# A two-layer decoder step on one core: a planner that tells a tile's first user from its writer, one more attention unit turned through DRAM, and output tiles entered between projections

## The chip, the core and the metric

The kernel runs on one core of a Trainium2 chip. The metric is the time on the device in microseconds (us), as the median of several executions. TensorE (PE) multiplies matrices out of SBUF into PSUM; VectorE (DVE), ScalarE (ACT) and GpSimd (POOL) work elementwise; SyncE (SP) issues nearly all transfers (DMAs), one behind the other in the order in which the program gives them.

## The reference

One inference step of a decoder for a prompt of 512 tokens and, with the same weights, for 8 sequences of one new token each, so 520 columns in all; the model width is 1024. The first layer is a gated linear recurrence (HGRN2, 16 heads of 128), the second is sliding-window attention (window 128, 32 query heads of 64, 4 key/value heads, partial rotary, a sink per head). Cut to what matters here:

```
# layer 0
u = rmsnorm(h, pre0) @ w_in_a;  q, f, i, z = split(u, 4)
o = hgrn2(silu(q), log f, 1 - f, i, S0)        # per head, chunked scan, final states are outputs
mix = (rmsnorm(o) * silu(z)) @ w_out_a
h = h + rmsnorm(mix, post0);  h = h + (p0 @ w_pe0) * sigmoid(h @ w_pg0)
# layer 1
k, v = split(rmsnorm(h, kvg) @ w_kv);  q, z = split(rmsnorm(h, pre1) @ w_in_b)
s = q k^T / 8, only keys of the last 128 positions;  pr = softmax([s, sink])[..., :-1]
mix = (pr v * silu(z)) @ w_out_b
h = h + rmsnorm(mix, post1);  h = h + (p1 @ w_pe1) * sigmoid(h @ w_pg1)
```

The outputs are h for both groups, the recurrent states, and the new key and value rows. All is float32; a product with a weight is made of three passes in the rounded format fp32r (high part of the weight by the high part of x, low part by high, high by low).

## The kernel before, in words

**Tiles.** A weight matrix is cut into tiles of 128 output rows. A tile is `kc` steps (8 for a projection) of six matmuls, for the two halves of 260 columns and the three passes. Weights arrive as `wr` (512 KB, 3 buffers); ACT rounds half of one to `wh`, and DVE or POOL makes the rest `wl`. Projection results stand in `pj` (2 pairs of PSUM banks), all else in `ph` (4 banks).

**Stages.** Embedding products; layer 0's 16 heads with four projections each (`proj_a`), each followed by that head's recurrence (`hgrn`), which runs beside the next heads' projections; after some heads a group's eight output tiles (`out_tiles`, groups in `GROUPS_A`: heads 0 to 3 after head 6, heads 4 to 7 after head 10, and so on). The last group goes by halves of the columns, and each half ends in a sum of squares `acc`, which `rstd` (L714) turns into the factors `R`: PE sums `acc` over the rows (`ones,acc`), DVE and POOL make `rsm` and `rsr`, PE spreads it by three or two transposes (`ident,rsr`), ACT copies it to `R`. `residual` (L777) then makes h and its parts `xs`, on which the `gates` tiles wait (weights `w_pg`). Layer 1 has eight units of four query heads: two query tiles and two gate tiles each (`unit_proj`), then the attention (`unit_attn`) beside the next units' projections, and groups of output tiles (`GROUPS_B`: units 0 and 1 after unit 4, units 2 and 3 after unit 5, units 4 and 5 after unit 7, then 6, then 7). It ends like layer 0.

**Attention of one unit** (`block`, L1327), in four blocks of 128 queries. W holds the scores, then the normalised weights (a buffer `b`, of the tags `b2` and `b3` with 3 buffers each). W has to be turned, queries to keys. For most units PE does that with four transposes into a bank, ACT rounds the bank to `hi`, DVE subtracts to get `lo`. For the units in `TURN_W` (4 and 5) `turn_weights` (L1414) does it: two DVE transposes of 32 by 32 blocks, one DMA to DRAM (`tw`), four DMAs back into W. In blocks 1 to 3 `hi` and `lo` are multiplied by a mask into two more tiles `ys`; in all units but the last two DMAs then move halves of the second into the first.

**Order.** Nothing is issued as it is written. `Plan.enter` (L187) records each operation with what it must follow; `Plan.issue` (L233) then builds the program by a list schedule with modelled costs: at each step the engine that can begin first takes, among the operations that are ready by the model, one by level (MAIN, SIDE, FIRST) and by its number in the written order. Operations further than `WINDOW`, for DMAs `LOADS`, from the lowest one that is not yet issued have to wait. The order in which each engine works is thus fixed before the run; on the chip an engine waits at each instruction for what it really needs. All instructions carry one line, that of the helper that calls them (L192).

`enter` makes an operation follow every earlier one that wrote a part of a tile which it reads or overwrites. It also makes each user of a tile follow the tile's first user, `self.maker[t]` (L211), whose output may be another part of the tile; `issue` counts that as a wait until the first user has ended, for a DMA until it has landed.

Of the kernel before, what the change touches and what calls it, by code (L numbers as in the profile page):

```python
# [9 lines left out]
F32 = mybir.dt.float32  # L10
F32R = mybir.dt.float32r
# [10 lines left out]
SEQ = 512  # L22
# [17 lines left out]
PIECE = 4 * P  # L40
SPLITS = 4
TURN_K, TURN_O = range(0, 15), range(1, 15)
TURN_W = (4, 5)
WARM = 17
BEHIND = 4

# [3 lines left out]
MAIN, SIDE, FIRST = 0, 1, 2  # L50
# [44 lines left out]
class Plan:  # L95
# [91 lines left out]
    def enter(self, on, name, a, k):  # L187
        outs = [k["accum_out"]] if "accum_out" in k else []
        outs.append(a[0])
        ins = [x for x in (*a, *k.values()) if isinstance(x, bass.AP)]  # L190
        calls = [getattr(getattr(self.nc, e), name) for e in on]
        op = Op(len(self.ops), self.level, on, [lambda c=c: c(*a, **k) for c in calls],  # L192
                [self.price(e, name, ins, a, k) for e in on], on[0] == "sync")
        if any(x.tensor.name.startswith("tw") for x in ins[1:]):
            op.late = LATE
        self.ops.append(op)
        for x in ins:
            t = x.tensor.name
            r = self.region(x)
            op.deps.update(o for q, o in self.writes.get(t, ()) if self.meet(q, r))  # L200
            self.reads.setdefault(t, []).append((r, op))
            kept = t in self.homes or x.space != bass.MemoryType.DRAM
            if kept and t not in self.left:
                tag, bufs = self.homes.get(t, (t, 1))
                if tag not in self.slots:
                    self.slots[tag] = Slots(tag, bufs)
                self.slots[tag].order.append(t)
                op.news.append((tag, t))
                self.maker[t] = op
            elif kept:  # L210
                op.deps.add(self.maker[t])  # L211
            if t not in op.tiles and kept:
                op.tiles.add(t)
                self.left[t] = self.left.get(t, 0) + 1
        for x in outs:
            t = x.tensor.name
            r = self.region(x)
            if on[0] == "tensor":
                r = 0, P, r[2] // 512 * 512, -(-r[3] // 512) * 512
            for book in (self.writes, self.reads):  # L220
                old = book.get(t, [])
                op.deps.update(o for q, o in old if o is not op and self.meet(q, r))
                book[t] = [(q, o) for q, o in old if o is op or not self.within(q, r)]
            self.writes.setdefault(t, []).append((r, op))
        op.deps.discard(op)
        op.load = op.dma and not op.deps
        for d in op.deps:
            d.users.append(op)
        op.open = len(op.deps)
        return op  # L230


    def issue(self):  # L233
# [3 lines left out]
        given, pipe, lanes, low, port, slow = set(), 0.0, [0.0] * 8, 0, 0.0, 0.0  # L237
        best = dict.fromkeys(clock)
        stale = set(clock)

        def after(d, e):

            if d.dma:
                return d.end + 0.1
            return d.end + (SAME if d.engine == e else LAT)[d.engine]

        def ready(op, e):
            return max((after(d, e) for d in op.deps), default=0.0)

        def place(op):  # L250
            at = 0.0
# [9 lines left out]
        def choose(e):  # L261
            able = []
            for op, r in wait[e]:
                p = place(op) if op.n < low + (LOADS if op.dma else WINDOW) else None
                if p is not None:
                    held = port if op.cost[op.on.index(e)][1] else 0.0
                    if op.dma and op.load and clock[e] > CALM and pipe > BACKLOG + op.cost[0][0]:
                        held = pipe - BACKLOG - op.cost[0][0]
                    able.append((max(r, p, clock[e], held), op, max(r, p)))
            if not able:  # L270
                return None
            t = min(x[0] for x in able)
            rank = RANK.get(e, OTHER)
            able = [x for x in able if x[0] <= t]
            safe = SAFE if t > CALM and low < self.second else 0.0
            fresh = lambda op: any(d.dma and d.end + safe > t for d in op.deps)
            able.sort(
                key=lambda x: (
                    e == "tensor" and x[2] + HAND > t or e in SHY and fresh(x[1]), rank[x[1].level], x[1].n
                )  # L280
            )
            if e == "gpsimd":
                for x in able:
                    op = x[1]
                    if len(op.on) > 1:

                        free = [
                            o.cost[0][0]
                            for o, r in wait["vector"]
                            if r <= t and not o.cost[0][1] and place(o) is not None  # L290
                        ]
                        if max(clock["vector"] - t, 0.0) * (port <= t) + sum(free) < op.cost[1][0]:
                            continue
                    return x
                return None
            return able[0]
# [6 lines left out]
        while todo:  # L303
# [11 lines left out]
            if op.n == low:  # L315
                while low < len(self.ops) and self.ops[low].engine:
                    low += 1
                stale.update(clock)
            cost, held = op.cost[n]
            if op.dma:  # L320
                t = max(t, lanes[0])
# [69 lines left out]
def in_turn(tiles):  # L391

    for t in tiles[1::2]:
        t.apart = True
    return tiles


def bank_of(ps, h):
# [56 lines left out]
class Step:  # L455
# [871 lines left out]
    def block(self, u, st, n, osb):  # L1327
# [52 lines left out]
                nc.tensor.matmul(po, base[0][:, kvh % 2], w, start=x == 0, stop=x == 1)  # L1380
        else:

            ys = [self.g_(F32R, SEQ) for x in range(2)]
            by = lambda x: x.rearrange("p (i h t) -> p i h t", h=4, t=run)
            mask = spot(self.tmask, 0, (run, P // run), (0, 4), (1, run))
            for x, y in zip((hi, lo), ys):
                nc.either.tensor_tensor(by(y), by(x.bitcast(F32)), mask, op=ALU.mult)
            y, z = (x.bitcast(F32) for x in ys)
            if u < 7:
                nc.sync.dma_start(y[HD:, : 4 * HD], z[:HD, : 4 * HD])  # L1390
                nc.sync.dma_start(y[:HD, 4 * HD :], z[HD:, 4 * HD :])
# [158 lines left out]
    def run(self):  # L1550
# [66 lines left out]
        def done_a(h):  # L1617
# [6 lines left out]

            return f

        for h in range(HEADS):
            tiles += self.proj_a(h, xg if h == 0 else xn, sts[h], done_a(h), R0 if h == 0 else None)
            if h + 1 in groups:
                tiles += out_a(h + 1)  # L1630
        tiles += out_a(17)
        end = out_a(18) + self.embed(0, pe[0], range(E0, KC), kept[0]) + self.embed(1, pe[1], range(E1))

# [47 lines left out]
        for u in range(8):  # L1681
            def done(u=u):
                self.beside(lambda: self.unit_attn(u, us[u]))
                if u % 4 == 3:
                    self.beside(lambda: self.sample_out(u // 4, us[u - 3 : u + 1]), FIRST)

            mine = self.unit_proj(u, qx, us[u], done)
            if u == 7:

                tiles[-2:-2] = mine[:2]  # L1690
                mine = mine[2:]
            tiles += mine
            if u + 1 in ogroups:
                tiles += out_b(u + 1)
        tiles += out_b(9)
        end1 = out_b(10) + self.embed(1, pe[1], range(E1, KC), kept[1])

# [143 lines left out]
```

## Time and profile before

| what | us |
|---|---|
| median of 3 runs | 1068.3 |
| lowest and highest of them | 1067.65, 1070.68 |
| the profiled execution's own time | 1068.61 |
| its span, first to last instruction | 1066.8 |
| PE busy, as the profile models it | 1057.2 |
| DVE busy | 904.7 |
| ACT busy | 681.8 |
| POOL busy | 114.0 |

Matmuls overlap in their pipeline, so that a row's mean duration (285 ns for most) is no cost; the distance from one start to the next is. Idle time of an engine counts only where the end of the program waits for it. Rows are grouped by what is written and read (`pj<-xs,wh`), with buffer numbers left out.

### The profile page before, as it was taken

To read this page: it belongs to the slowest core of one execution; us is meant where nothing else is said; L and a number is where in the kernel's file an instruction comes from. 1 tells how busy PE (TensorE), PEld (TensorE's weight loads), DVE (VectorE), ACT (ScalarE), POOL (GpSimd) and SP (SyncE) were. 2 spreads that over 40 slices of the span, in tenths; PEclk is the share of its full clock that TensorE was granted. 3 is DMA by queue.
4 is the path that set the end of the run, shared out by engine and by line. 5 is a ranking of instruction groups with operands and counts; after the bars stand their busy time and mean duration, and the time that the engine had idled before them with its cause. 6 is when DMAs were issued, how large, how long until landed. Compare 5 with 4: busy or idle time off the path is not lost.

```text
span 1066.8 us, 23981 instructions
## 1 busy us (share of the span) xinstructions
PE 1057.2 (99%) x8828; PEld 1051.2 (99%) x8828; DVE 904.7 (85%) x1963; ACT 681.8 (64%) x1829; POOL 114.0 (11%) x198
## 2 busy tenths in 40 slices
PE   9999999999999999999999999999999999999998
PEld 8999999999999999999999999999999999999998
DVE  8899788875787958788889999699999998999894
ACT  7877676655767637776636565477667664675542
POOL 1111121101111112111111000000100000002000
PEclk9999999999999999999999999999999999999999
DMA  9556586665646646576663454544433545423432
GB/s 314 183 190 183 143 247 195 191 195 156 213 155 206 193 130 224 177 210 191 190 223 142 159 190 142 170 121 136 124 101 115 164 155 186 154 82 124 156 100 81
DMA packets 147069, 178.99 MB, mean 168 GB/s; under 512 B 76932, under 2 KB 99660, under 8 KB 146952
## 3 DMA queue, kind: packets, MB, share of 16 engines
q1 hardware_dynamic: 146952, 177.46, 52.7%
q8 instruction: 70, 1.15, 0.4%
q14 instruction: 47, 0.39, 0.1%
HBM read 137.04 MB, written 34.86 MB: 161 GB/s over the span
## 4 chain that ended last, share of the span: by engine, by line
PE 91%; ACT 4%; DVE 3%; issue 1%; DMA 0%; POOL 0%; DVEq 0%; POOLq 0%
PE pj L192 71%; PE ph L192 21%; ACT g L192 1%; ACT wh L192 1%; DVE wl L192 1%; DVE x L192 0%; DMA wr<-in_w_pg 0%; ACT tmp L192 0%; ACT sb L192 0%; ACT b L192 0%; DVE acc L192 0%; ACT og L192 0%; DVE xr L192 0%; DVE tmp L192 0%; DVE g L192 0%
## 5 line engine op out<-in xcount | busy, mean ns | idle before, releaser
L192 PE MATMUL pj<-xs,wh 128*128 128x260 f32 (+2 forms) x3264 | 554.7, 285 | 1.6 <-ACT xs L192 1.3
L192 PEld LDWEIGHTS pj<-xs,wh 128*128 128x128 f32 x3264 | 457.7, 189 | 3.2 <-ACT xs L192 2.3
L192 PE MATMUL pj<-xs,wl 128*128 128x260 f32 (+2 forms) x1632 | 340.5, 285 | 0.0
L192 PEld LDWEIGHTS pj<-xs,wl 128*128 128x128 f32 x1632 | 255.1, 188 | 0.2
L192 ACT CAST wh<-wr 128x512 fp32r<-128x512 f32 x287 | 176.2, 619 | 111.1 <-PE pj L192 100.5
L192 DVE TENSOR_TENSOR wl<-wr,wh 128x512 fp32r<-128x512 f32 x275 | 187.6, 685 | 48.6 <-ACT wh L192 47.4
L192 PE MATMUL pj<-og,wh 128*128 128x260 f32 x1056 | 182.4, 285 | 0.3 <-ACT og L192 0.3
L192 PEld LDWEIGHTS pj<-og,wh 128*128 128x128 f32 x1056 | 149.5, 188 | 0.9 <-ACT og L192 0.5
L192 PE MATMUL pj<-og,wl 128*128 128x260 f32 x512 | 106.3, 284 | 0.1
L192 PEld LDWEIGHTS pj<-og,wl 128*128 128x128 f32 x512 | 79.9, 188 | 0.3 <-DVE wl L192 0.3
L192 ACT ACTIVATE sb<-sb,g 128x128 f32<-128x128 f32 x128 | 64.7, 556 | 2.4 <-DVE sb L192 2.4
L192 ACT ACTIVATE sb<-sb,nv 128x128 f32<-128x128 f32 x128 | 63.1, 555 | 0.3
L192 ACT COPY b<-ph 128x256 f32<-128x256 f32 (+1 forms) x80 | 27.8, 350 | 47.0 <-PE ph L192 46.5
L192 ACT ACTIVATE b<-b,an 128x129 f32<-128x129 f32 x128 | 50.6, 398 | 4.5 <-DVE an L192 4.4
L192 ACT ACTIVATE tmp<-pj 128x520 f32<-128x520 f32 (+2 forms) x48 | 24.5, 527 | 43.3 <-PE pj L192 43.2
L192 PE MATMUL ph<-xs,b 128*128 128x256 f32 (+1 forms) x360 | 50.5, 283 | 0.0
L192 DVE COPY_PREDICATED xr<-lmask,ph 128x256 f32<-128x256 int32 x96 | 46.8, 487 | 3.8 <-PE ph L192 3.4
L192 PE MATMUL ph<-xr,b 128*128 128x128 f32 x320 | 49.0, 275 | 0.3 <-ACT b L192 0.3
L192 DVE TENSOR_TENSOR x<-x,pj 128x520 f32<-128x520 f32 (+2 forms) x64 | 39.5, 621 | 10.8 <-PE pj L192 10.2
L192 DVE TENSOR_TENSOR g<-g,b 128x256 f32<-128x256 f32 x96 | 40.5, 422 | 9.3 <-ACT b L192 6.1
L192 DVE TENSOR_TENSOR xr<-xr,b 128x256 f32<-128x256 f32 x96 | 41.0, 427 | 8.6 <-PE ph L192 6.4
L192 PEld LDWEIGHTS ph<-xs,b 128*128 128x128 f32 x360 | 46.3, 188 | 0.1
(222 smaller groups left out, 1737.8 us busy)
## 6 DMA issues: line engine op xcount, KB each, us to landing
wr<-in_w_in_a SPq DMA_DIRECT2D x64, 512.0 KB, 4.5
sb<-sd SPq DMA_DIRECT2D x32, 512.0 KB, 4.5
wr<-in_w_in_b SPq DMA_DIRECT2D x32, 512.0 KB, 4.0
td<-tmp SPq DMA_DIRECT2D x45, 256.0 KB, 3.2
xr<-td SPq DMA_DIRECT2D x180, 64.0 KB, 3.2
sb<-in_state SPq DMA_DIRECT2D x16, 512.0 KB, 5.4
out_st_s<-sb SPq DMA_DIRECT2D x16, 512.0 KB, 3.0
wr<-in_w_out_a SPq DMA_DIRECT2D x16, 512.0 KB, 4.8
```

Source lines behind the costliest of these rows:

```text
L192: op = Op(len(self.ops), self.level, on, [lambda c=c: c(*a, **k) for c in calls], [self.price(e, name, ins, a, k) for e in on], on[0] == " ...
```

## The change

Six edits. (1) Unit 3 joins `TURN_W`. (2) In all units but the last, the masked `lo` is written into W's own place instead of a tile of the tag `g`. (3) `enter` keeps the first user apart as `op.soft` if it wrote nothing that the operation reads: it still has to be issued earlier, but `ready` and `fresh` no longer wait for its end. (4) In layer 1, how far ahead a weight load may be issued is counted from the first TensorE operation of level MAIN that is not yet issued, and no longer from the lowest operation of any kind. (5) The output tiles of the groups after heads 6 and 10 are entered two at a time behind each projection tile of heads 7 and 11 (`weave`, `WEAVE_A`). (6) The same could be done in layer 1, but `WEAVE_B` is empty.

```diff
-TURN_W = (4, 5)
+TURN_W = (3, 4, 5)
+WEAVE_A, WEAVE_B = (7, 11), ()
...
+        makers = set()
...
             elif kept:
-                op.deps.add(self.maker[t])
+                makers.add(self.maker[t])
...
         op.deps.discard(op)
+        op.soft = makers - op.deps - {op}
+        op.deps |= op.soft
...
+        main, front = [op for op in self.ops if op.level == MAIN and "tensor" in op.on], 0
...
         def ready(op, e):
-            return max((after(d, e) for d in op.deps), default=0.0)
+            return max((after(d, e) for d in op.deps if d not in op.soft), default=0.0)
...
-                p = place(op) if op.n < low + (LOADS if op.dma else WINDOW) else None
+                first = main[front].n if op.load and op.level == MAIN and front < len(main) and low >= self.second else low
+                p = place(op) if op.n < first + (LOADS if op.dma else WINDOW) else None
...
-            fresh = lambda op: any(d.dma and d.end + safe > t for d in op.deps)
+            fresh = lambda op: any(d.dma and d.end + safe > t for d in op.deps if d not in op.soft)
...
+def weave(mine, out):
+
+    n = -(-len(out) // len(mine))
+    return [x for k, t in enumerate(mine) for x in (t, *out[k * n : (k + 1) * n])]
...
-            ys = [self.g_(F32R, SEQ) for x in range(2)]
+            ys = [self.g_(F32R, SEQ), spot(home, 0, (1, SEQ)) if u < 7 else self.g_(F32R, SEQ)]
...
+        out = []
         for h in range(HEADS):
-            tiles += self.proj_a(h, xg if h == 0 else xn, sts[h], done_a(h), R0 if h == 0 else None)
-            if h + 1 in groups:
-                tiles += out_a(h + 1)
+            tiles += weave(self.proj_a(h, xg if h == 0 else xn, sts[h], done_a(h), R0 if h == 0 else None), out)
+            out = out_a(h + 1) if h + 1 in groups else []
+            if h + 1 not in WEAVE_A:
+                tiles += out
+                out = []
```

Since the planner's rules change, the order moves on every engine from the first stage on. Counted over the whole program PE has 16 instructions fewer, all of them transposes `ph<-ident,b`; DVE has 8 more stream transposes, SP 20 more DMAs (4 `tw<-tmp`, 16 `b<-tw`). Six `b<-b,ad` products and six more `wl` subtractions stand on POOL, and five mask products fewer.

**Unit 3, block 1.** On PE before, W is `b_2043_2137`, the bank of the turned W `ph_2144`:

```order
L192 MATMUL pj_2217<-xs_1725,wh_2209 128x260
L192 MATMUL ph_2163<-xr_1788,g_2093 128x256
L192 MATMUL ph_2163<-xr_1792,g_2093 128x256
L192 MATMUL ph_2163<-xr_1788,g_2094 128x256
L192 MATMUL ph_2163<-xr_1792,g_2094 128x256
L192 MATMUL ph_2144<-ident,b_2043_2137 128x2x64 x4
L192 MATMUL pj_2217<-xs_1725,wh_2209 128x260
```

On SP in the change, W of block 1 is `b_2035_2129`, of block 2 `b_2047_2141`, of block 3 `b_2059_2153`; `wr` are weight loads, `qd` belongs to the next unit's queries:

```order
L193 DMA tw_2137<-tmp_2136 128x512
L193 DMA wr_2283<-in_w_out_b 128x1024
L193 DMA tw_2149<-tmp_2148 128x512
L193 DMA g_2197<-qd_2199 64x512
L193 DMA g_2198<-qd_2199 64x512
L193 DMA b_2035_2129<-tw_2137 32x4x128 x4
L193 DMA b_2047_2141<-tw_2149 32x4x128 x3
L193 DMA wr_2292<-in_w_in_b 128x1024
L193 DMA b_2047_2141<-tw_2149 32x4x128
L193 DMA tw_2161<-tmp_2160 128x512
L193 DMA g_2139<-b_2035_2129 64x256 x2
L193 DMA b_2059_2153<-tw_2161 32x4x128 x4
```

The four transposes on PE are gone; in SP's queue stand the way through DRAM and, between it and the next weight loads, the move of the masked half out of W.

**The end of layer 0.** On DVE, `x` are the sums of the output tiles, `acc_1506` the sum of squares, whose last part for the first half of the columns is the row with `tmp_1518`. Before:

```order
L192 TENSOR_TENSOR acc_1506<-acc_1506,tmp_1514 128x256
L192 TENSOR_TENSOR x_724<-x_724,pj_1556 128x264
L192 TENSOR_TENSOR acc_1506<-acc_1506,tmp_1517 128x256
L192 TENSOR_TENSOR wl_1562<-wr_1560,wh_1561 128x512
L192 TENSOR_TENSOR acc_1506<-acc_1506,tmp_1518 128x256
L192 TENSOR_TENSOR acc_1506<-acc_1506,tmp_1557 128x264
```

In the change:

```order
L193 TENSOR_TENSOR acc_1506<-acc_1506,tmp_1517 128x256
L193 TENSOR_TENSOR x_726<-x_726,pj_1556 128x264
L193 TENSOR_TENSOR acc_1506<-acc_1506,tmp_1518 128x256
L193 TENSOR_TENSOR x_731<-x_731,pj_1556 128x264
L193 TENSOR_TENSOR wl_1562<-wr_1560,wh_1561 128x512
L193 TENSOR_TENSOR x_744<-x_744,ph_1558 128x264
```

The subtraction `wl_1562` has moved behind the last part of the sum. The subtraction `wl_1568`, which stood on POOL at this place, now stands on DVE further down, and PE's row that reads `acc_1506` stands 17 matmuls earlier.

**The end of layer 1.** On PE, `ident,rsr` spreads the second half's factor; the gates read `xs`. Before:

```order
L192 MATMUL ph_2805<-xs_2715,b_2702_2796 128x256
L192 MATMUL ph_2762<-ident,rsr_2761 128x128 x3
L192 MATMUL pj_2792<-xs_2717,wh_2755 128x256
L192 MATMUL pj_2792<-xs_2717,wh_2779 128x256
L192 MATMUL pj_2792<-xs_2717,wl_2756 128x256
```

In the change:

```order
L193 MATMUL ph_2788<-xs_2697,b_2685_2779 128x256 x2
L193 MATMUL ph_2745<-ident,rsr_2744 128x128 x3
L193 MATMUL pj_2775<-xs_2698,wh_2738 128x256
L193 MATMUL pj_2775<-xs_2698,wh_2762 128x256
L193 MATMUL ph_2788<-xs_2698,b_2685_2779 128x256
L193 MATMUL pj_2775<-xs_2700,wh_2738 128x256
```

Three matmuls on the first `xs` pair have moved behind the transposes, ahead of the first row that reads the second pair (`xs_2717`, now `xs_2700`).

More of the change, by code (lines that the diff above doesn't have):

```diff
@@ L318, in issue @@
                 stale.update(clock)
+            while front < len(main) and main[front].engine:
+                front += 1
+                stale.add("sync")
             cost, held = op.cost[n]
@@ L1387, in block @@
                 nc.either.tensor_tensor(by(y), by(x.bitcast(F32)), mask, op=ALU.mult)
-            y, z = (x.bitcast(F32) for x in ys)
+            y, z = (x.bitcast(F32) if x.dtype == F32R else x for x in ys)
             if u < 7:
@@ L1691, in run @@
                 mine = mine[2:]
-            tiles += mine
-            if u + 1 in ogroups:
-                tiles += out_b(u + 1)
+            tiles += weave(mine, out)
+            out = out_b(u + 1) if u + 1 in ogroups else []
+            if u + 1 not in WEAVE_B:
+                tiles += out
+                out = []
         tiles += out_b(9)
```

## The prediction

> **What bounds the kernel now.** I read the page first: the busy shares, then the chain that ended last.
>
> ```profile
> span 1066.8 us, 23981 instructions
> PE 1057.2 (99%) x8828; PEld 1051.2 (99%) x8828; DVE 904.7 (85%) x1963; ACT 681.8 (64%) x1829; POOL 114.0 (11%) x198
> PE 91%; ACT 4%; DVE 3%; issue 1%; DMA 0%; POOL 0%; DVEq 0%; POOLq 0%
> ```
>
> PE is nearly never idle and carries the chain. But a modelled busy PE can hide late starts, so the next view is the busy time by stretches, where the count of matmuls in a stretch tells its pace (columns: stretch, its length, then busy us and count of PE, weight loads, DVE, ACT, POOL, then clock, DMA share, GB/s).
>
> ```profile
> 0.00:125.00 125.00, 122.25 (x1002) 119.78 (x1003) 107.98 (x228) 93.18 (x213) 20.09 (x51) 1.00 0.64 208
> 125.00:250.00 125.00, 125.00 (x1057) 124.86 (x1057) 99.21 (x213) 82.56 (x212) 16.40 (x29) 1.00 0.66 198
> 575.00:600.00 25.00, 23.72 (x188) 22.68 (x189) 25.00 (x64) 14.47 (x37) 1.72 (x2) 1.00 0.62 221
> 600.00:650.00 50.00, 50.00 (x419) 49.98 (x419) 47.22 (x124) 31.90 (x85) 2.00 (x2) 1.00 0.36 124
> 800.00:850.00 50.00, 50.00 (x416) 49.67 (x415) 45.83 (x97) 36.81 (x120) 2.60 (x2) 1.00 0.45 138
> 1000.00:1025.00 25.00, 23.87 (x198) 23.37 (x197) 24.32 (x64) 16.86 (x40) 2.53 (x2) 1.00 0.32 109
> ```
>
> In the undisturbed stretches PE makes 1057 matmuls in 125 us and 416 to 419 in 50: one in 0.119 us, at full clock. Measured by that pace 22 matmuls are missing at the end of layer 0 (575 to 600: 25 / 0.119 = 210, there are 188), which is 2.6 us; 12 at the end of layer 1, 1.4 us; 48 in the first 125 us, 5.7 us, of which the first microsecond and the warm-up are a part that no edit touches. That is all there is to win beside PE's own work: about 10 us, in three places. Within the two layers there is nothing, and the list of PE's waits says the same: none lies between 125 and 560 us, and between 600 and 985 us there is one, for `ad`.
>
> ```profile
> PE pj L192 <- ACT xs L192: 1.3, 2, 0.8
> PE ph L192 <- DVE far L192: 1.1, 1, 1.1
> PE ph L192 <- DVE acc L192: 0.5, 1, 0.5
> PE ph L192 <- POOL rsr L192: 0.4, 1, 0.4
> PE ph L192 <- DVE ad L192: 0.2, 1, 0.2
> ```
>
> **The change part by part. Unit 3 through DRAM** takes 4 blocks of 4 transposes from PE. What one costs is seen in the timeline of unit 3, where PE's queue is full:
>
> ```profile
> 814.30 0.64 PE L192 MATMUL pj<-og,wh 128*128 128x260 f32 x4
> 814.78 0.40 PE L192 MATMUL pj<-og,wl 128*128 128x260 f32 x2
> 815.02 0.60 PE L192 MATMUL ph<-ident,b 128*128 128x128 f32 x4
> 815.37 0.72 PE L192 MATMUL pj<-og,wh 128*128 128x260 f32 x4
> 815.93 0.40 PE L192 MATMUL pj<-og,wl 128*128 128x260 f32 x2
> ```
>
> Four wide matmuls take 814.78 - 814.30 = 0.48 us. From 815.02 to 815.93 there are four transposes and four wide matmuls, 0.91 us, so the transposes are 0.43 us, 0.108 each; 16 of them are **-1.7 us**. This is certain as far as PE stays full, and no more than 16 x 0.273 = 4.4 us could come of it even if each held PE for its whole duration, which the rows exclude. In their place come, with the nearest rows:
>
> ```profile
> L192 PE MATMUL ph<-ident,b 128*128 128x128 f32 x96 | 14.7, 273 | 0.2 <-DVE ad L192 0.2
> L192 DVE STREAM_TRANSPOSE tmp<-b 128x256 f32<-128x256 f32 x16 | 6.8, 430 | 0.1
> L192 DVE TENSOR_TENSOR b<-b,ad 128x512 f32<-128x512 f32 x32 | 22.0, 686 | 0.6
> L192 DVE TENSOR_TENSOR g<-g,tmask 128x512 fp32r<-128x512 f32 x40 | 26.8, 684 | 0.1
> L192 POOL TENSOR_TENSOR wl<-wr,wh 128x512 fp32r<-128x512 f32 x12 | 15.7, 1308 | 215.6 <-ACT wh L192 148.4 <-DMA qd<-g 44.8 <-DVE g L192 22.4
> L192 SPq DMA_DIRECT2D b<-tw x32: 303/430/584, 831.6 to 904.2; - x32
> tw<-tmp SPq DMA_DIRECT2D x8, 256.0 KB, 2.9
> b<-tw SPq DMA_DIRECT2D x32, 64.0 KB, 3.5
> g<-g SPq DMA_DIRECT2D x42, 64.0 KB, 2.0
> ```
>
> DVE: 8 x 0.430 = 3.4 us, against 4.2 us idle in 800 to 850 (45.83 busy), where unit 3 runs. SP: 20 issues of 0.43, 8.6 us of queue. Latency: 2.9 + 4 x 0.43 + 3.5 = 8.1 us per block, where PE and ACT took under one. The cover: in the new order unit 3's last attention matmul stands 269 matmuls ahead of the first output tile that needs the unit, 269 x 0.119 = 32 us. If that cover were gone, each block would show up to 8 us on PE. Units 4 and 5 already go this way in 827 to 904 us, and PE has no wait there. I take **+0.3**, for small waits among more queued DMAs (bounds 0 and +6, the latter below under the slower rival).
>
> **Masked parts in W's place** adds and removes no instruction; a `g` tile is freed, and W is held until its two moving DMAs have landed: a cast, a subtraction and two mask products of 0.69 each, two issues and 2.0 us of landing, some 6 us longer. `b3` takes two blocks of each unit on three buffers, a unit lasts at least 192 x 0.119 = 23 us, so the next user is not kept. Nothing. The mask products that go from POOL back to DVE (5 x 0.684 = 3.4 us) are outweighed by the `b<-b,ad` products that go the other way (6 x 0.686 = 4.1 us).
>
> **First-user rule and load window** change no work, only the order. In `turn` and `turn_weights` the planner no longer waits for the first of four landings, so it counts on results some 3 us sooner; on the chip the four were issued without that wait before too (0.43 us each). A better order can only help where PE waits. At the end of layer 0:
>
> ```profile
> 573.45 1.46 POOL L192 TENSOR_TENSOR wl<-wr,wh 128x512 fp32r<-128x512 f32 x1 [17.61 <-ACT wh L192]
> 573.69 1.51 DVE L192 TENSOR_TENSOR acc<-acc,tmp 128x256 f32<-128x256 f32 x1
> 575.25 0.60 PE L192 MATMUL ph<-ones,acc 128*128 128x1 f32 x4 [0.50 <-DVE acc L192]
> 589.83 0.50 PE L192 MATMUL pj<-xs,wh 128*128 128x256 f32 x2 [0.50 <-ACT xs L192]
> 572.75 0.41 DVE L192 TENSOR_TENSOR acc<-acc,tmp 128x256 f32<-128x256 f32 x1
> ```
>
> The same sum takes 0.41 us alone and 1.51 beside a POOL subtraction, and PE waits for it. In the new order that subtraction is on DVE (0.7) and one more stands behind the sum, so DVE, busy for 25.00 of 25 us here, saves 1.1 - 0.7 = 0.4 us, PE no longer waits 0.5 us for `acc` except for what its own earlier place costs (17 matmuls, 2.0 us, against 0.7 + 1.1 us that the sum comes sooner). The gates then wait for `xs` by DVE's pace. Bounds: 0, and the stretch's whole 2.6. I take **-0.7**, nearer to what DVE saves, since DVE sets this stage.
>
> At the end of layer 1:
>
> ```profile
> 1016.14 0.54 PE L192 MATMUL ph<-ident,rsr 128*128 128x128 f32 x3 [0.36 <-POOL rsr L192]
> 1017.45 0.51 PE L192 MATMUL pj<-xs,wh 128*128 128x256 f32 x2 [0.77 <-ACT xs L192]
> ```
>
> Three matmuls now lie between the transposes and the row that waited 0.77 us: 3 x 0.119 = 0.36. The wait for `rsr` stays. **-0.3** (bounds 0 and -1.1).
>
> **Woven output tiles** move 8 + 8 tiles among projections in a stretch (125 to 400 us) where PE is full and DVE has 26 of 125 us free. Nothing to win; if DVE lacked that room, each tile's addition (0.7 us) would be late. 0. The first stage's order is nearly as before: 0, within one microsecond either way.
>
> Sum: -1.7 - 0.7 - 0.3 + 0.3 = -2.4 us on the profiled execution's 1068.61 (span 1066.8, so 1.8 us lie around it), that is 1066.2 with a span of 1064.4. That execution was 0.3 above the median of the runs, 1068.3, so the median becomes **1065.9**.
>
> **The rivals.** *A larger gain:* the planner's truer waits fill the three places. If half of the 2.6 + 1.4 and 2 of the first stretch's 5.7 us go, the sum is -1.7 - 2.0 - 2.0 = -5.7 with no new waits, 1062.6. For it: one rule was wrong for 45 turns (180 DMAs) of layer 0. Against: the places with the largest waits are bound by DVE or by a chain with nothing beside it.
>
> *DVE takes it back, no change:* six more normalisations and six more subtractions go to POOL. If each holds a DVE addition as in the rows at 573 us (1.1 us), less the mask and other products that leave POOL (five, and six small ones at half), DVE loses 12 x 1.1 - 8 x 1.1 = 4.4 us, beside 3.4 for the turns, against 4.2 idle in 50 us. Some 2 to 3 us of it would reach PE through the `pj` pairs: 1068.3 - 2.4 + 2.4 = 1068.3. Against: in 600 to 650 us DVE is at 47.22 of 50 and PE loses nothing. The Trainium skill ("GPSIMD Engine Reference", section Specifications) says that GpSimd's SBUF interfaces are shared with VectorE and contend with its instructions of two SBUF inputs; the sum at 573.69 us is such an instruction and agrees.
>
> *Slower, by SP's queue:* the move `g_2139<-b_2035` waits on SP for a chain of landing, cast, subtraction and two products (3.5 + 0.6 + 3 x 0.69 = 6.2 us), and weight loads queue behind it. PE takes its matmuls in a fixed order, so a masked half that lands late stops it. In unit 3 this decides once SP runs more than one tile (48 x 0.119 = 5.7 us) behind the plan; three masked blocks, each some 2.5 us late, then cost 7.5 us: 1065.9 + 7.5 = 1073.4. Against: the same pattern in units 4 and 5.
>
> **How the numbers follow.** Forecast 0.50, larger gain 0.22, no change 0.16, slower 0.12. A measurement of this kernel can tell 0.3% (3.2 us, below 1065.1 or above 1071.5) from no change. The larger gain (0.22) and some 0.14 of the forecast's 0.50 lie below 1065.1: faster 0.36; slower 0.12; within 0.3% the rest, 0.52. The range of 8 in 10 runs from 1062.4, which leaves out the lower part of the larger gain, to 1069.6, which holds the no-change case and leaves out the slower one.
>
> **What would show it.** Right: 80 transposes `ph<-ident,b` instead of 96; 416 or more matmuls per 50 us from 600 to 985 us; no POOL subtraction beside `acc` and no wait of PE for `acc` over 0.3 us; over 190 matmuls in the 25 us at the end of layer 0; the wait for `xs` at the end of layer 1 near 0.4. Wrong: PE waits in layer 1 on DMA-moved `g` or on `wh`; fewer than 414 matmuls per 50 us there; DVE above 49 of 50 us with PE short.

## The result and the profile after

The changed kernel takes 1073.23 us (median of 9 runs, 1071.34 to 1074.78), the kernel before 1068.58 beside it (9 runs, 1067.56 to 1070.97): 1.0041 times as long, 95% interval 1.0032 to 1.0050. The forecast was 1065.9, the range 1062.4 to 1069.6. The profiled execution of after is, with one other, the fastest of the nine: 1071.34 us with a span of 1069.2, that is 2.4 us more span than before. The other 2 us are in the executions that this profile does not show; later profiles of the same order show in part where. A small part lies outside the span: the nine executions take 2.0 to 3.1 us more than their spans, the profiled one of before 1.8. Why is not known.

Of the page of after: span, busy shares, chain.

```profile
span 1069.2 us, 24042 instructions
PE 1057.6 (99%) x8812; PEld 1050.1 (98%) x8812; DVE 909.5 (85%) x1970; ACT 684.4 (64%) x1829; POOL 120.8 (11%) x199
PE 90%; ACT 4%; DVE 3%; DMA 2%; SPq 1%; issue 1%; DVEq 0%; ACTq 0%
```

16 matmuls are gone and nothing else of PE's work has changed; DVE and POOL are busy longer by 4.8 and 6.8 us. The busy time by stretches tells where the time went. First the two stretches of before that the prediction did not show, then six of after (columns as in the prediction).

```profile
700.00:750.00 50.00, 50.00 (x418) 49.79 (x417) 47.82 (x95) 34.42 (x109) 3.88 (x3) 1.00 0.43 131
750.00:800.00 50.00, 50.00 (x423) 49.86 (x422) 47.00 (x107) 34.15 (x115) 4.42 (x4) 1.00 0.38 114
```

```profile
575.00:600.00 25.00, 24.42 (x201) 23.81 (x200) 24.77 (x62) 16.08 (x40) 1.72 (x2) 1.00 0.65 223
650.00:700.00 50.00, 49.05 (x406) 48.33 (x404) 41.46 (x89) 28.05 (x82) 1.81 (x2) 1.00 0.57 165
700.00:750.00 50.00, 48.87 (x405) 48.37 (x406) 47.49 (x93) 33.35 (x102) 5.34 (x4) 1.00 0.42 130
750.00:800.00 50.00, 48.80 (x406) 48.10 (x405) 47.64 (x106) 33.88 (x120) 9.56 (x8) 1.00 0.34 107
800.00:850.00 50.00, 49.87 (x414) 49.53 (x413) 46.00 (x98) 35.33 (x108) 1.04 (x1) 1.00 0.57 173
1000.00:1025.00 25.00, 24.57 (x202) 23.88 (x201) 24.36 (x63) 16.92 (x41) 2.09 (x2) 1.00 0.40 138
```

Both ends of layers have gained: 201 matmuls instead of 188, 202 instead of 198. The loss stands where before had none. From 700 to 800 us before makes 418 + 423 = 841 matmuls, after 811: 30 are missing, at 0.119 us 3.6 us; 11 more between 650 and 700 (406 against 417). And POOL's busy time in 750 to 800 us has doubled, from 4.42 to 9.56. PE's waits in layer 1:

```profile
PE ph L193 <- DVE g L193: 1.9, 2, 1.1
PE ph L193 <- ACT g L193: 0.5, 1, 0.5
PE ph L193 <- ACT b L193: 0.4, 1, 0.4
PE ph L193 <- DMA g<-qd: 0.4, 1, 0.4
```

The two long ones (0.83 and 1.05 us) are for `g` of DVE, the low part `lo` of a turned block. The timeline of after around the first of them, DVE, then POOL, then PE:

```profile
697.57 0.67 DVE L193 TENSOR_TENSOR g<-ph,g 128x512 fp32r<-128x512 f32 x1
698.17 1.81 DVE L193 TENSOR_TENSOR tmp<-tmp,tmp 128x520 f32<-128x520 f32 x1
699.91 0.68 DVE L193 TENSOR_TENSOR g<-ph,g 128x512 fp32r<-128x512 f32 x1
...
698.14 1.29 POOL L193 TENSOR_TENSOR g<-g,tmask 128x512 fp32r<-128x512 f32 x1 [42.87 <-ACT g L193]
...
700.64 0.38 PE L193 MATMUL ph<-g,x 128*128 128x256 f32 x1 [0.83 <-DVE g L193]
```

POOL's mask product starts 0.03 us ahead of DVE's addition `tmp<-tmp,tmp` (a part of the rotary embedding), which then takes 1.81 us instead of the 0.68 to 0.70 of its like; the subtraction behind it (`g<-ph,g`) is 1.1 us late, and PE waits for it. Around the second long wait it is a subtraction `wl` on POOL, and on DVE the second of two products of one row:

```profile
761.42 2.38 DVE L193 TENSOR_TENSOR og<-ao,og 128x512 fp32r<-128x512 f32 x2
763.73 0.68 DVE L193 TENSOR_TENSOR g<-ph,g 128x512 fp32r<-128x512 f32 x1
...
761.69 1.56 POOL L193 TENSOR_TENSOR wl<-wr,wh 128x512 fp32r<-128x512 f32 x1 [4.13 <-issue]
...
764.46 0.50 PE L193 MATMUL ph<-g,x 128*128 128x512 f32 x1 [1.05 <-DVE g L193]
```

**Why POOL starts there.** `issue` knows of this conflict. Its variable `port` keeps the end of the last operation that the model counts as a user of a port which DVE and POOL share (a DVE operation that reads two SBUF tiles, or copies or scales one of them into SBUF, and nearly everything on POOL). The next such operation may begin in the plan only at `max(r, p, clock[e], held)`, with `held = port`. But this is a wait of the plan's clock alone. The program makes POOL wait for its inputs and for nothing else. For each of the 17 products that the plan of after gives to POOL in layer 1, the plan says how long it is held by the port, and the trace what it met:

```
start in the plan, held there | start on the chip, product | DVE instruction beside it that ran long
692.65  1.98 | 698.14 g<-g,tmask | tmp<-tmp,tmp 1.81
694.55  0.77 | 702.97 b<-b,ad    | b<-g,tmask 1.43
722.07  0.31 | 731.45 wl         | none
747.55  1.00 | 756.15 b<-b,ad    | ao<-ao,g 1.53
752.17  0.31 | 761.69 wl         | og<-ao,og 1.78
758.09  0.41 | 769.34 b<-b,ad    | none
784.95  1.76 | 795.60 b<-b,ad    | tmp<-tmp,m 1.54
870.43  1.00 | 881.84 b<-b,ad    | ao<-ao,g 1.53
974.63  1.62 | 985.76 g<-g,tmask | wl 1.19
the 8 others, held 0          | one: tmp<-tmp,bd 1.17
```

Seven of nine held products meet a DVE instruction that runs 0.5 to 1.1 us too long, one of the eight others does. Before has 15 such products in layer 1, of which the plan holds two, by 0.4 us, and no DVE instruction beside them takes over 0.76. This is a correlation; the experiments test it.

### The profile page after: what moved, and what is told of

The parts are those of the page before. It is cut to its first block, busy times and chain, and to the rows that moved or that the text cites. A ratio compares the mean times of both kernels' runs of the same rounds, so it can differ in the third digit from the quotient of the medians.

```text
span 1069.2 us, 24042 instructions
## 1 busy us (share of the span) xinstructions
PE 1057.6 (99%) x8812; PEld 1050.1 (98%) x8812; DVE 909.5 (85%) x1970; ACT 684.4 (64%) x1829; POOL 120.8 (11%) x199
## 4 chain that ended last, share of the span: by engine, by line
PE 90%; ACT 4%; DVE 3%; DMA 2%; SPq 1%; issue 1%; DVEq 0%; ACTq 0%
PE pj L193 69%; PE ph L193 21%; DVE tmp L193 1%; SPq L193 1%; DMA g<-qd 1%; ACT sb L193 1%; ACT wh L193 1%; ACT g L193 1%; ACT b L193 1%; DMA x<-in_xT 0%; DMA qd<-g 0%; ACT tmp L193 0%; DVE ao L193 0%; DVE g L193 0%; ACT og L193 0%
## 5 line engine op out<-in xcount | busy, mean ns | idle before, releaser
L193 DVE TENSOR_TENSOR wl<-wr,wh 128x512 fp32r<-128x512 f32 x269 | 184.8, 689 | 52.0 <-ACT wh L193 50.8
L193 PE MATMUL pj<-og,wh 128*128 128x260 f32 x1056 | 186.0, 285 | 0.5 <-ACT wh L193 0.3
L193 POOL TENSOR_TENSOR wl<-wr,wh 128x512 fp32r<-128x512 f32 x18 | 24.2, 1342 | 253.9 <-ACT wh L193 229.9
L193 ACT COPY b<-g 128x256 f32<-128x256 f32 (+1 forms) x112 | 40.8, 378 | 15.5 <-DVE g L193 12.7
```

## The experiments

Every time is a median, beside runs of the kernel before on the same chip (their medians lie between 1068.28 and 1068.80). "Planned anew" means that an edit changes the whole order behind it; the other edits leave each engine's order as it is.

**Products off POOL.** `e2` makes copies on ACT of all 17 products, `e9` of the nine held ones, `e10` of the eight others.

```diff
+        if len(on) > 1:
+            op.alt = lambda: self.nc.scalar.copy(a[0], a[1])
...
-            self.tc.keep_in_program_order(op.calls[n]())
+            away = n == 1 and len(op.on) > 1 and low >= self.second      # e9: and held > 0.2; e10: and held <= 0.2
+            self.tc.keep_in_program_order(op.alt() if away else op.calls[n]())
```

> The changed kernel in its own order, but each product and subtraction that the plan gives to POOL in layer 1 (17 of them: subtractions wl, normalisations and mask products) is a copy on ACT of the same tile at the same place in the order, so POOL has no wide work there; the multiplication or subtraction itself is left out. Theory B (POOL's work beside DVE's two-input work makes the loss): DVE's instructions of 1.43 to 1.81 us at 698, 703, 756, 762, 781 and 795 us go back to 0.43 to 0.69, PE's waits of 1.1 us at 699.5 and 1.3 at 763.1 go, and 2.5 to 4 us of the 5 lost between 650 and 850 us come back: 1069 to 1070.5. Theory A (a chain from the table load): the wait at 694.3 stays, those behind it shrink in part, 1070 to 1071.5. Theory C (SP's queue and late landings): the waits stay, 1073.

> The changed kernel in its own order; of the 17 products that the plan gives to POOL in layer 1 only those 9 become copies on ACT (their arithmetic left out) that in the plan were ready 0.3 to 2.0 us before POOL takes them, held back there until DVE's two-input instruction has ended. On the chip nothing holds them: POOL starts when the inputs are there, beside that instruction. Theory (held products make the loss): nearly the whole gain of the run with all 17 off, 3.2 us, comes back, to 1070.0 to 1070.5, and DVE's instructions of 1.4 to 1.8 us go except for the one at 781. Rival (POOL's work costs DVE wherever it stands): about half of it, 1071.7.

> The counterpart: the other 8 products, which the plan lets POOL start as soon as their inputs are there, become copies on ACT (arithmetic left out); the 9 held ones stay on POOL. Theory (held products): the waits at 699 and 763 us stay, 1072.5 to 1073.5, at most the one long DVE instruction at 781 us goes. Rival (wherever it stands): about half of 3.2 us comes back, 1071.5.

Measured: `e2` 1070.01 (1.0009 of before, 1.0000 to 1.0018), `e9` 1070.60 (1.0023, 1.0014 to 1.0031), `e10` 1073.26 (1.0046, 1.0034 to 1.0058). The stretches 700 to 800 us of the three, in this order:

```profile
700.00:750.00 50.00, 50.00 (x418) 49.68 (x417) 47.45 (x95) 36.54 (x107) 0.00 (x0) 1.00 0.47 138
750.00:800.00 50.00, 50.00 (x422) 49.91 (x421) 46.94 (x112) 39.69 (x136) 0.20 (x1) 1.00 0.37 110
```

```profile
700.00:750.00 50.00, 49.99 (x419) 49.68 (x417) 47.45 (x94) 35.49 (x106) 2.58 (x2) 1.00 0.47 139
750.00:800.00 50.00, 50.00 (x420) 49.71 (x419) 47.20 (x112) 37.88 (x132) 4.42 (x5) 1.00 0.37 109
```

```profile
700.00:750.00 50.00, 48.67 (x403) 47.95 (x402) 47.45 (x93) 33.59 (x102) 2.90 (x3) 1.00 0.44 132
750.00:800.00 50.00, 48.91 (x408) 48.41 (x408) 47.29 (x108) 35.92 (x125) 5.68 (x5) 1.00 0.36 109
```

Without the held products PE makes 839 matmuls there, as many as without all (840) and nearly as many as before (841); without the others 811, as after. The other products on POOL cost nothing that shows there. In the whole time, by the ratios, `e9` gets back 1.9 of the 3.4 us that `e2` does, not nearly all as expected. Its profile lacks 10 matmuls between 600 and 650 us (409 against 419 in after), where PE waits 0.9 us for `acc`. That wait stands in `e3` below too, where all 17 products are off, so it is not the other products' doing. These kernels also leave arithmetic out and relieve POOL of up to 17 products of 1.04 to 1.69 us, so the next one leaves nothing out.

**A real wait.** Ahead of each held product POOL multiplies one column of the DVE result for which the plan held it, and so has to wait for that instruction.

```diff
+            if n == 1 and len(op.on) > 1 and low >= self.second and best[e][0] - best[e][2] > 0.2:
+                self.tc.keep_in_program_order(self.hold(self.wide))
             self.tc.keep_in_program_order(op.calls[n]())
+            if e == "vector" and op.cost[n][1] and op.out.shape[0] == P and op.out.start_partition() == 0:
+                self.wide = op
...
+        self.plan.hold = lambda op: self.tc.nc.gpsimd.tensor_tensor(dm, col(op.out), self.mhalf[:, :1], op=ALU.mult)
```

> The changed kernel with nothing left out, and a real wait where the plan only counts one: ahead of each of the 9 held products POOL multiplies one column of the DVE result that the plan lets end first, so that POOL starts where the plan says. All other engines keep their order. Theory (a product that the plan holds and the chip doesn't makes the loss): DVE's instruction behind which POOL was held runs in 0.4 to 0.7 us again, the waits at 699 and 763 us go or shrink to under 0.4, and most of what the run with these 9 off got back comes back, 1070.5 to 1071.5; less of it where the next instruction of DVE has two inputs too and now runs beside POOL instead. Rival (a product on POOL costs DVE the same wherever it starts): nothing, 1073.

Measured: 1069.62 (1.0009, 1.0001 to 1.0018), 3.6 us faster than after with nine instructions more and every engine's order kept. Its timeline at the first held product:

```profile
699.44 0.70 DVE L193 TENSOR_TENSOR tmp<-tmp,tmp 128x520 f32<-128x520 f32 x1
...
702.02 0.19 POOL L584 TENSOR_TENSOR dm<-g,mhalf 128x1 f32<-128x1 f32 x1 [46.03 <-DVE g L193]
702.17 1.30 POOL L193 TENSOR_TENSOR g<-g,tmask 128x512 fp32r<-128x512 f32 x1
```

The mask product starts 2.7 us behind DVE's addition instead of beside it, the addition takes 0.70 us, and between 600 and 985 us PE no longer waits for any `g` of DVE. No DVE instruction beside a held product runs long any more; the one long one left is beside one of the eight others (0.94 us at 779). PE makes 418 + 419 = 837 matmuls in 700 to 800 us. That the missing wait was the cause is thereby shown, for 3.4 to 3.6 of the 4.6 us.

**The table load.** The first softmax of layer 1 needs another table of functions on ACT, which the plan does not know of. `e1` brings the load forward; `e3` does the same to `e2`, `e14` to the kernel with the real wait.

```diff
                 nc.scalar.activation(hi[:, :SEQ], q[:, :SEQ], AF.Copy, scale=-SCALE)
+                if u == 0 and c == 0:   # issued right behind this one, outside the plan
+                    self.plan.warm = lambda: self.tc.nc.scalar.activation(self.dm, self.lb[:, :1], AF.Exp)
```

> The changed kernel with one instruction more: an exponential of one column on ACT right behind the first query's copy of layer 1 (673 us in the trace of after), where ACT idles for 1.4 us. The table load of 1.28 us, which stands in the trace of after at 689.23 ahead of the first softmax, goes there; every other instruction keeps its place. Theory A (the loss of the change is a chain that begins where the first block's softmax is late; the table load is its start, and what follows, DVE's products beside POOL's at 698 and 703, only happens because POOL and DVE have slipped against each other): PE's wait of 0.39 us at 694.3 goes and with it most of the waits to 715, the matmuls of 650 to 750 us rise from 811 to some 830, and the time falls by 2 to 3 us, to about 1070.5. Theory B (POOL's products hold DVE's wherever they meet, whatever came before): only the wait at 694.3 goes, 0.5 us, about 1072.7. Theory C (SP's queue and the landings make the loss): nothing, 1073.2.

> The changed kernel with the table load early and POOL's 17 products of layer 1 as copies on ACT (their arithmetic left out): the two edits before together. Theories A and B: only the wait for the query halves at 685 us (0.5) and the one at 835 us (0.3) stay, the lost 5 us come back but for one, 1068.5. Theory C: 1073.

> The changed kernel with POOL's real wait and the table load early, all else in its order. With POOL's products back where the plan has them, the late softmax is the last delay at 694 us that the plan does not know: 0.5 to 1 us under the run with the wait alone, 1068.6 to 1069.1. If the softmax's delay is hidden by the wait for the query halves at 686 us, no gain: 1069.6.

The load in after, and in `e1`:

```profile
689.23 1.28 ACT L193 ACT_TABLE_LOAD   x1
```

```profile
674.05 1.28 ACT L1292 ACT_TABLE_LOAD   x1
```

Alone it brings nothing to the time: 1073.14 (1.0036, 1.0023 to 1.0050). Theory A is right on the stretch and wrong on the time: PE's wait at 694 us is gone, the first product no longer holds up DVE's addition, and 650 to 750 us have 414 + 413 = 827 matmuls instead of 811. But the later products still meet DVE (405 matmuls in 750 to 800 us), 9 matmuls fewer than in after stand between 800 and 900 us, and among PE's waits in this profile is a new one, at 835 us, for a moved masked half:

```profile
PE ph L193 <- DMA g<-b: 0.8, 1, 0.8
```

With the products off it is 1069.59 (1.0007, 0.9999 to 1.0016), 0.4 below `e2` and not told apart from it. Behind the real wait it brings 1.0 us: 1068.62 (1.0000, 0.9991 to 1.0008). The interval overlaps that of `e12`, but the profiles agree: 414 matmuls in 650 to 700 us, where `e12` has 405. So after, with nine short waits and one early table load, takes the time of before.

**The first-user rule alone**, on the kernel before, and with the real wait:

```diff
-                op.deps.add(self.maker[t])
+                makers.add(self.maker[t])
...
+        op.soft = makers - op.deps - {op}
+        op.deps |= op.soft
```

> The kernel before with the first-user rule alone (units 4 and 5 through DRAM, masked parts in their own tile, old load window, nothing woven). The plan then gives POOL 11 products in layer 1, 8 of them held, 7.0 us together (before: 2 held, 0.8 together), though the plan ends within 0.1 us of before's. Theory of the held products: 2 to 4 us slower than before, 1071 to 1072.5, with DVE instructions of 1.2 to 1.8 us beside them, and waits at about 194 us for a landing that the plan now counts on sooner. Rival (the loss needs unit 3 or the masked parts): as before, 1068.5.

> The kernel before with the first-user rule alone, as in the run of that name, and a real wait of POOL ahead of each of the 8 held products of layer 1. If the held products are all that the rule costs, the 4.3 us come back and the end of layer 0 stays better: 1068 or less. If the rule also costs in layer 0 (waits for turned tiles at 141, 189 and 218 us in that run's profile, 2.1 us of PE's time there), only layer 1's part comes back, 2 to 2.5 us: 1070.5, and those waits stay.

Measured: 1072.86 (1.0040, 1.0026 to 1.0054) and 1069.13 (1.0006, 0.9997 to 1.0015). The rule alone makes as large a loss as the whole change, and the wait takes 3.7 us of it back. No usable profile of the second is on record, so whether its waits in layer 0 stayed is not seen. Among PE's waits in the profile of the first:

```profile
PE ph L193 <- DVE g L193: 0.8, 1, 0.8
PE ph L193 <- DMA xr<-td: 0.6, 2, 0.5
```

The second is in layer 0, for a tile turned through DRAM. In the order of after the row that reads such a tile at 195 us waits 1.03 us in the profile of `e5` below and 0.70 in that of `e2`, whose programs are the same as after's up to there, and not at all in that of after; nor does it wait in the profiles of before and of `e6`, which lacks the rule. The timeline of `e5`:

```profile
195.88 1.13 PE L193 MATMUL ph<-xr,xr 128*128 128x128 f32 x8 [1.03 <-DMA xr<-td]
```

By the stretch 125 to 250 us, `e5` and `e2` make 1047 matmuls and the rule alone 1041, where before makes 1057 and after 1059. So the rest of the loss, one to two microseconds that come and go between executions of one order, is at least in part here.

**Each other edit taken away** from the change, planned anew: `TURN_W = (4, 5)` (`e4`), masked parts in a tile of their own (`e5`), no first-user rule (`e6`), `first = low` (`e7`), `WEAVE_A = ()` (`e8`).

> The changed kernel with unit 3 turned on PE again (16 transposes more on PE, 20 DMAs and 8 stream transposes fewer); its order is planned anew. If the longer turn of unit 3 or its DMAs make the loss between 685 and 840 us (theory C), that goes: 1073.2 - 5 + 1.7 = 1070. If the loss is the phase of POOL's and DVE's work in units 0 to 2 (A or B), which do not go through DRAM, it stays where those collisions stay: 1075, with 14 products on POOL in layer 1 instead of 17 perhaps 1073.

> The changed kernel, but the masked parts take a tile of their own again instead of W's place. The order is planned anew from the second block of unit 0 on. The plan then gives 13 products of layer 1 to POOL; of the 6 that are held there, those at 692.7 and 694.6 us of the plan stay as they are, four more stand at 737 (0.2), 846 (2.3), 982 (1.0) and 1000 (0.8). If W held for longer makes the loss, layer 1 is free of it: 1068.5. If the held products do, the waits between 694 and 715 us stay and those at 763 go: lost in 600 to 985 us some 3 to 4 us; the plan itself is 5 us longer at its end, so 1073 to 1077.

> The changed kernel without the first-user rule (a first user's place in the order counts as a wait again), the whole order planned anew. 12 products of layer 1 on POOL, 5 of them held by 1.0 to 2.0 us, at 748, 758, 798, 847 and 912 us of the plan. If the first-user rule makes the planner count on results too soon and so makes the loss, it goes: 1067 to 1069. If the held products make it, some 3 to 5 us stay lost between 750 and 920 us: 1071 to 1075.

> The changed kernel without the load window edit: the order is the same up to 804 us of the plan, and of the held products those of units 0 to 2 stay. If the edit only moves loads that nobody waits for, as predicted, nothing changes: 1073. If it helps or hurts, the difference lies behind 804 us.

> The changed kernel with the output tiles of groups 7 and 11 entered whole again; the order differs between 174 and some 420 us and in layer 1 hardly at all (the same 9 held products). If the woven tiles cost nothing, as predicted, the time stays at 1073.2; the wait at 194 us for a turned tile (0.7 to 1.3 us in some profiles of the changed order) shows whether it comes with them or with the first-user rule.

```
       us       of before  interval
e4  1076.28      1.0070    1.0057 to 1.0083
e5  1081.49      1.0122    1.0108 to 1.0137
e6  1076.00      1.0077    1.0064 to 1.0091
e7  1073.78      1.0051    1.0037 to 1.0065
e8  1072.54      1.0037    1.0023 to 1.0050
```

The load window and the woven tiles make no difference that can be told (after is at 1.0041). The profile of `e8` has waits for turned tiles at 190 and 219 us, so these do not come with the woven tiles. In `e4`, where PE has the 16 transposes again, the wait at 763 us stays (1.05 us, now at 766), as the held-product theory wants, but the one at 699 us is not in its profile. The same product starts beside the same addition, and this time POOL is the one held up (1.88 us), as in the profile of `e8` too (1.89). POOL and DVE in `e4`:

```profile
700.29 1.88 POOL L193 TENSOR_TENSOR g<-g,tmask 128x512 fp32r<-128x512 f32 x1 [42.82 <-ACT g L193]
...
700.32 0.69 DVE L193 TENSOR_TENSOR tmp<-tmp,tmp 128x520 f32<-128x520 f32 x1
```

So the same instructions in the same order cost DVE 1.1 us in one execution and, by its next two-input instruction (1.19 us instead of 0.68), 0.5 in another. `e5` and `e6` are worse than I expected by either theory: both are orders whose own plan ends 5 us later than after's. `e6` loses next to nothing up to 800 us, although its plan holds two products by 1.8 and 1.9 us before then: a held product costs the end only where PE waits for what stands behind it. Then PE waits elsewhere, for a rounding on ACT:

```profile
PE ph L193 <- ACT g L193: 2.5, 2, 2.2
```

An edit that is planned anew thus says little about itself alone, and these five cannot be added up.

**A version from the findings**: the change without the first-user rule, the table load early, the first output group of layer 1 woven too, and POOL takes a product of layer 1 only if the port is free when its inputs are there.

```diff
-                        if max(clock["vector"] - t, 0.0) * (port <= t) + sum(free) < op.cost[1][0]:
+                        if low >= self.second and t > x[2] + 0.05 or max(clock["vector"] - t, 0.0) * (port <= t) + sum(free) < op.cost[1][0]:
```

> A version that follows from the runs: the change without its first-user rule (unit 3 through DRAM, masked parts in W's place, load window, woven tiles stay, and the output tiles of layer 1's first group are woven too), the table load early, and POOL takes a product in layer 1 only if the port is free when its inputs are there (8 products, none held). Its plan ends 1.2 us sooner than before's. If the held products and the table load were the loss, the plan now holds on the chip as before's does: 1068.6 - 1.2 - 0.4 = 1067. If new waits on landings come with unit 3 (835 and 868 us), 1068 to 1070.

Measured: 1066.67 (0.9985, 0.9976 to 0.9995), faster than both kernels, than before by 0.15%. Its busy shares, and two stretches:

```profile
PE 1054.8 (99%) x8812; PEld 1049.3 (99%) x8812; DVE 911.1 (86%) x1984; ACT 683.8 (64%) x1830; POOL 100.8 (9%) x185
```

```profile
700.00:750.00 50.00, 50.00 (x420) 49.87 (x420) 46.53 (x91) 32.91 (x102) 1.35 (x2) 1.00 0.44 135
750.00:800.00 50.00, 50.00 (x422) 49.70 (x421) 48.40 (x108) 34.09 (x111) 1.50 (x2) 1.00 0.40 119
```

POOL has 20 us less to do than in after and DVE more than before, and PE is full in these stretches. It differs from `e6` by three edits at once, and they were not tried apart.

## Why the prediction was wrong

**Right.** The transposes: `ph<-ident,b` stands 80 times, and nothing in the runs speaks against 0.108 us of PE's time for each. The end of layer 0: -0.7 was forecast; 13 matmuls more are 1.5 us, twice that, the wait for `acc` is gone and the sum takes 0.42 us with no POOL subtraction beside it. The end of layer 1: -0.3 was forecast, 4 matmuls are 0.5 us, and the wait for `xs` has gone from 0.77 to 0.43; the wait for `rsr`, which was to stay, is not in this profile. Load window and woven tiles: 0, as measured.

The group row of the transposes in after, then its timeline: DVE's last part of the first half's sum, PE's rows that read it, and the gate's wait at the end of layer 1.

```profile
L193 PE MATMUL ph<-ident,b 128*128 128x128 f32 x80 | 12.3, 273 | 0.4 <-ACT b L193 0.4
```

```profile
572.94 0.42 DVE L193 TENSOR_TENSOR acc<-acc,tmp 128x256 f32<-128x256 f32 x1
573.85 0.50 PE L193 MATMUL ph<-ones,acc 128*128 128x1 f32 x4
1019.25 0.50 PE L193 MATMUL pj<-xs,wh 128*128 128x256 f32 x2 [0.43 <-ACT xs L193]
```

**The step that failed** is "First-user rule and load window change no work, only the order. ... A better order can only help where PE waits." The order also decides when POOL starts beside DVE, and that can hurt where PE did not wait before. I had the mechanism in hand: the sum of 0.41 us that takes 1.51 beside a POOL subtraction stands in the prediction, as a gain at the end of layer 0. I did not ask where the new order makes such meetings, though the rows of the order name the 17 products and the kernel's own plan, had its starts been read, names the nine that it holds and the chip doesn't. The prediction also counted nothing for PE's readers of tiles turned in layer 0, which wait at 190 to 219 us in some profiles with the rule and in none of the three without it (before, `e6`, and the last version).

**The small waits of layer 1** were put at +0.3 (bounds 0 and +6); they are 41 matmuls in 650 to 800 us, 4.9 us. Against the forecast the miss is 1073.23 - 1065.9 = 7.3 us; the real wait and the early table load take 4.6 of it back. The other 2.7 remain in `e14`, which keeps the transposes out and both layer ends as in after (200 and 202 matmuls): against before its profile lacks 17 matmuls, 2.0 us, in 125 to 250, 600 to 650 and 800 to 850 us (1050, 416 and 409 against 1057, 419 and 416). What they wait for in each execution was not settled. Of the signs named for "wrong", fewer than 414 matmuls per 50 us (405 and 406) and a wait for moved `g` (0.4 us) both came; DVE above 49 of 50 us did not (47.64), and need not: the loss is not a shortage of DVE's time but its phase.

**The rival "DVE takes it back"** (0.16, 1068.3) had the cause and not the size. It counted products (12 more, 8 fewer) at 1.1 us each and let a part of the net reach PE. What counts is which of them start in the middle of DVE's work: 8 of the 17, with some 6 us of DVE's time, of which the real wait gets 3.6 us of the end back. Its argument against, that in 600 to 650 us DVE is at 47.22 of 50 and PE loses nothing, was no argument: in before the first product of layer 1 on POOL starts at 700.83 us.

**The rival "slower, by SP's queue"** came to the right time, 1073.4, by luck: it put the loss into unit 3, after 800 us, where the profile of after is short of 2 matmuls (414 against 416). The waits that it foresaw exist, 0.8 us at 835 us in `e1`, and belong to the microseconds that come and go.

**Masked parts in W's place**: "nothing" holds for W's next user: no wait of PE for it shows in the profile of after. But with the tile of its own back, the newly planned order is 8 us slower than after, so the freed tile may well be what lets this order exist. How much of the 8 us is the tile and how much the order was not separated.

Open stays how much the layer 0 waits cost on average, and what each of the last version's edits brings.

## What to carry to other kernels

Where a list scheduler models a conflict between two engines (a shared port, a bandwidth), compare the start it plans with the moment at which the inputs are there: each difference that no semaphore enforces is a place where the chip will do something else, and a short real wait there can be worth more than the work that was moved. Read a changed order not only for what PE waits on, but for which instructions now run beside each other. And delays in a row can hide each other: taking one away (the table load) showed nothing in the time until the other was gone.

## What the runs showed of the hardware

**DVE and POOL hold each other up for a whole instruction.** At 698 us DVE's addition begins 0.03 us after POOL's product and ends 1.81 us later: what is left of the product, 698.14 + 1.29 - 698.17 = 1.26, and then 0.55 of its own. At 761 us it is POOL that starts in the midst of DVE's product and takes 1.56 us instead of 1.29. So does this subtraction in after, which delays nobody:

```profile
731.31 0.68 DVE L193 TENSOR_TENSOR og<-ao,og 128x512 fp32r<-128x512 f32 x1
...
731.45 1.69 POOL L193 TENSOR_TENSOR wl<-wr,wh 128x512 fp32r<-128x512 f32 x1 [2.09 <-DVE tmp L193]
```

The Trainium skill ("SBUF — State Buffer", section "SBUF: two separate sides") says just this: an exclusive lock, held by the one that starts first for its whole instruction, against DVE instructions with two SBUF inputs; the trace agrees, in both directions, where the starts lie a tenth of a microsecond or more apart. At 0.03 us the recorded starts do not tell who will wait: in after it was DVE, in `e4` POOL. The long DVE row at 781 us is of another kind, a TENSOR_SCALAR that reads one tile and a factor for each row and that `issue` does not count for `port`; it takes 1.17 us there and 0.27 in before. One group row for each kernel shows what POOL itself loses, first after, then the kernel with the real wait:

```profile
L193 POOL TENSOR_TENSOR b<-b,ad 128x512 f32<-128x512 f32 x6 | 7.3, 1222 | 108.9 <-DVE ad L193 89.1 <-ACT b L193 19.8
```

```profile
L193 POOL TENSOR_TENSOR b<-b,ad 128x512 f32<-128x512 f32 x6 | 6.2, 1041 | 2.8 <-DVE ad L193 2.7
```

So the price of a product on POOL is no constant: here between nothing and 1.1 us of DVE's time, by when it starts. Not expected either was how much one order varies: the wait for the turned tile in layer 0 was between 0 and 1.03 us in profiles whose program is the same up to there.
